# A 90-degree rotation on one core: in twelve macro tiles, two neighbouring outputs are stored by one 4 MB transfer

## The chip, the core and the metric

The kernel runs on one core of a Trainium2 chip. The metric is the time of one launch in microseconds (us); lower is better. A core has five engines with instruction streams of their own: TensorE (PE in the profile; its weight loads are PEld), VectorE (DVE), ScalarE (ACT), GpSimd (POOL) and SyncE (SP). Transfers between DRAM and the on-chip memory SBUF are carried by 16 DMA engines, whichever engine issued them. An engine that issues a transfer goes on; the transfer adds 16 to a semaphore when all of it has landed.

## The reference

```python
def setup_inputs():
    return {"x": np.random.randn(8192, 8192).astype(np.float32), "k": 1}

def reference(x, k):
    return np.rot90(x, k)
```

With k = 1 this is a transpose with the order of the rows reversed: out[i, j] = x[j, 8191 - i]. Nothing is calculated; 268 MB are read and 268 MB written.

## The kernel before

The input is cut into 16 macro tiles of 1024 rows by 4096 columns. Macro tile kk is read by eight loads (T = 8), one for each group of 128 rows: 128 partitions with 16 KB each, 2 MB in all. It leaves as eight outputs (J = 8, numbered j), each of 512 columns of the input, that is 512 rows of the result by 1024 columns: 128 partitions with 4 rows of 4 KB each, 2 MB again. Load number m is row group m % 8 of macro tile m // 8, output n is number n % 8 of macro tile n // 8; there are 128 of each. In the last macro tile alone an output covers 4 row groups and 1024 columns, and is written in rows of 2 KB.

Every step has an engine of its own.

- SyncE issues the loads. The first five go to the five buffers of 16 KB per partition; later, two of them (LAND = 2) receive loads and three (OUTS = 3) hold outputs. Load m waits until VectorE has emptied the buffer that it goes to.
- VectorE (line 209) waits for the load to land (line 203) and copies the tile, with the columns of each block reversed, into a ring of 63 slots of 2 KB per partition. The ring holds one macro tile less one slot, so a tile can be copied only after the outputs of the macro tile before have freed its slots: load m needs output m - 8 to be transposed (`s_half`), and for its last block the beginning of output m - 7 (`s_first`).
- TensorE (line 241) transposes 128 by 128 blocks from the ring into PSUM. The PSUM tensors `ps0` and `ps1` hold one half of an output each; a half is used again once ScalarE has copied it (`s_ev`). The first output of each macro tile, j = 0, needs all eight loads; its transposes are ordered by row group, so that it follows the loads as they land.
- ScalarE (line 272) copies the two halves of an output into its output buffer, having waited, before the first half, until the last store from that buffer has landed (line 268). It then issues the store itself (line 277).

The output buffers are used in turn, in ascending order: `LAND + (n + 1) % OUTS`. The last eight outputs go to all five buffers, as no loads are left by then.

`whole_reads` goes over the finished program: where a store's read of a partition is one contiguous stretch, it writes the access pattern as one run. So a store reads 16 KB runs and writes 4 KB rows.

Of the kernel before, what the change touches and what calls it, by code (L numbers as in the profile page):

```python
# [6 lines left out]
P = 128  # L7
# [3 lines left out]
T = R // P  # L11
W = 4096
G = 4
J = W // (G * P)
# [3 lines left out]
CH = G * P  # L18
F = G * R
# [4 lines left out]
H = 2  # L24
LAND = 2
OUTS = 3

LINE = 1024
HEAD = 224
# [20 lines left out]
def slot(kk, t, j):  # L50

    at = t * J + j if kk % 2 == 0 else J + t + j * T
    return (at + kk // 2 * (J + 1)) % SLOTS


def kernel(tc: tile.TileContext, x: bass.AP, k: bass.AP, out: bass.AP):
    nc = tc.nc
# [4 lines left out]
    dt = x.dtype  # L62
    macros = [(r0, c0) for r0 in range(0, N, R) for c0 in range(0, M, W)]
    KK = len(macros)
    n_out = KK * J
# [18 lines left out]
    with tc.tile_critical():  # L84
        head = nc.alloc_sbuf_tensor("head", [P, HEAD], dt)
        ident, scratch = head[:, :P], head[:, P : P + 1]
        bufs = [nc.alloc_sbuf_tensor(f"buf{i}", [P, F], dt) for i in range(LAND + OUTS)]
        ring = nc.alloc_sbuf_tensor("ring", [P, SLOTS * CH], dt)
        for b in bufs:
            assert nc.lookup_mloc(b).addr % LINE == 0  # L90
        ps = [
            nc.alloc_psum_tensor(f"ps{h}", [P, F // H], mybir.dt.float32)
            for h in range(H)
# [2 lines left out]
        s_id = nc.alloc_semaphore("s_id")  # L96
        s_land = [nc.alloc_semaphore(f"s_land{i}") for i in range(LAND + OUTS)]
        s_store = [nc.alloc_semaphore(f"s_store{i}") for i in range(LAND + OUTS)]
        s_rev = nc.alloc_semaphore("s_rev")
# [4 lines left out]
        def load_buf(m):  # L104
            if m < T:
                return m % (LAND + OUTS)
            return LAND + 2 if m == T else (m - T - 1) % LAND

        def out_buf(n):
            e = n - (n_out - J)  # L110
            if e < 0:
                return LAND + (n + 1) % OUTS
            ends = [load_buf(n_load - 2)]
            ends += [LAND + (n_out - J + i + 1) % OUTS for i in range(OUTS)]
            ends += [load_buf(n_load - 1)]
            return ends[e % len(ends)]

# [24 lines left out]
        def runs(kk, t, lo, hi):  # L142

            at = [slot(kk, t, j) for j in range(lo, hi)]
            i = 0
            while i < len(at):
                n = 1
                step = at[i + 1] - at[i] if i + 1 < len(at) else 1
                if step > 0:
                    while i + n < len(at) and at[i + n] - at[i + n - 1] == step:  # L150
                        n += 1
                else:
                    step = 1
                yield lo + i, n, at[i], step
                i += n

        def load(e, m):
            r0, c0 = macros[m // T]
            b = load_buf(m)
            e.dma_start(  # L160
                out=bufs[b][:], in_=x[r0 + m % T * P : r0 + (m % T + 1) * P, c0 : c0 + W]
            ).then_inc(s_land[b], 16)

        def uses_before(n_or_m, buf):
            return sum(buf(i) == buf(n_or_m) for i in range(n_or_m))
# [4 lines left out]
        with nc.Block() as block:  # L170

            @block.gpsimd
            def _(e):
                e.memset(ident, 0.0).then_inc(s_id, 1)  # L174
                e.wait_ge(s_id, 1)
                e.affine_select(  # L176
                    out=ident,
                    in_=ident,
                    compare_op=mybir.AluOpType.not_equal,
                    fill=1.0,  # L180
                    base=0,
                    pattern=[[-1, P]],
                    channel_multiplier=1,
                ).then_inc(s_id, 1)

            @block.sync
            def _(e):
                for m in range(LAND + OUTS, n_load):
                    last = [i for i in range(m) if load_buf(i) == load_buf(m)]
                    e.wait_ge(s_rev, rev[last[-1], J - 1])  # L190
                    load(e, m)
                for b in range(LAND + OUTS):
                    n = sum(out_buf(i) == b for i in range(n_out))
                    if n:
                        e.wait_ge(s_store[b], 16 * n)

            @block.vector
            def _(e):
                for m in range(n_load):
                    kk, t = divmod(m, T)  # L200
                    b = load_buf(m)
                    a = bufs[b][:].rearrange("p (j c) -> p j c", c=CH)
                    e.wait_ge(s_land[b], 16 * (uses_before(m, load_buf) + 1))
                    for lo, hi, wait in pieces[m]:
                        if wait:
                            e.wait_ge(*wait)
                        for j, n, at, step in runs(kk, t, lo, hi):
                            v = ring[:, at * CH : (at + (n - 1) * step + 1) * CH]
                            i = e.tensor_copy(  # L209
                                out=bass.AP(  # L210
                                    tensor=v.tensor,
                                    offset=v.offset,
                                    ap=[v.ap[0], [step * CH, n], [1, CH]],
                                ),
                                in_=a[:, j : j + n, ::-1],
                            )
                        i.then_inc(s_rev, 1)

            @block.tensor
            def _(e):  # L220
                seen = {}

                def wait(sem, n):
                    if seen.get(sem, 0) < n:
                        seen[sem] = n
                        e.wait_ge(sem, n)

                e.wait_ge(s_id, 2)
                for n, (kk, ts, js) in enumerate(outs):
                    blocks = [(j, g) for j in reversed(js) for g in range(G)]  # L230
                    half = len(blocks) // H
                    rows = len(ts) * P

                    def transpose(t, b):
                        j, g = blocks[b]
                        if n:
                            wait(s_ev, H * (n - 1) + b // half + 1)
                        wait(s_rev, rev[kk * T + t, j])
                        at = slot(kk, t, j) * CH + g * P
                        f = b % half * rows + (t - ts[0]) * P  # L240
                        i = e.transpose(  # L241
                            ps[b // half][:, f : f + P], ring[:, at : at + P], ident
                        )
                        if t == ts[-1] and b % half == half - 1:
                            i.then_inc(s_half, 1)
                        elif t == ts[0] and b == len(blocks) - 1:
                            i.then_inc(s_first, 1)

                    order = [(t, b) for b in range(len(blocks)) for t in ts]
                    if js[0] == 0:  # L250
                        order.sort()
                    for t, b in order:
                        transpose(t, b)

            @block.scalar
            def _(e):
                e.wait_ge(s_id, 2)
                e.copy(scratch, ident[:, :1])  # L258
                for n, (kk, ts, js) in enumerate(outs):
                    r0, c0 = macros[kk]  # L260
                    rows = len(ts) * P
                    b = out_buf(n)
                    for h in range(H):
                        if h == 0:
                            stores = uses_before(n, out_buf)
                            loads = [i for i in range(n_load) if load_buf(i) == b]
                            if stores:
                                e.wait_ge(s_store[b], 16 * stores)
                            elif loads:
                                e.wait_ge(s_rev, rev[loads[-1], J - 1])  # L270
                        e.wait_ge(s_half, H * n + h + 1)  # L271
                        e.copy(  # L272
                            bufs[b][:, h * F // H : (h + 1) * F // H], ps[h][:]
                        ).then_inc(s_ev, 1)
                    top = M - c0 - (js[-1] + 1) * CH
                    e.wait_ge(s_ev, H * (n + 1))
                    e.dma_start(  # L277
                        out=out[
                            top : top + len(js) * CH, r0 + ts[0] * P : r0 + ts[0] * P + rows
                        ].rearrange("(g m) f -> m g f", m=P),  # L280
                        in_=bufs[b][:].rearrange("m (g f) -> m g f", f=rows),
                    ).then_inc(s_store[b], 16)


# [33 lines left out]
```

## Time and profile before

| | |
|---|---|
| time, median of 3 runs | 1265.17 us (1265.15 to 1265.67) |
| the profiled execution's own time | 1265.5 us |
| its span | 1263.6 us |
| busy: PE, PEld, DVE, ACT | 693.0, 647.0, 402.9, 467.0 us |
| moved by DMA | 537.48 MB, mean 425 GB/s over the span |
| a load, from issue to landing | 16.8 us (median) |
| a store, from issue to landing | 25.7 us (median) |
| idle of VectorE, most of it waiting for loads | 812.1 us |
| idle of ScalarE, most of it waiting for stores | 778.2 us |

Times in the profile count from the start of the span. "Idle before" is the time in which an engine had nothing running just ahead of a group of instructions, and the arrow names what ended it. A busy engine is one with an instruction running; for a DMA engine, one with a packet under way. A packet is one read descriptor with the rows that it is written to; here a data packet has 16 KB and a semaphore packet 4 bytes. The queue q1 holds the loads issued by SyncE, q10 the stores issued by ScalarE. The trace lists each packet with its queue, start, duration and size; the prediction calls these packet records.

### The profile page before, as it was taken

The page shows a single profiled execution, that of the slowest core. Times are in us where ns is not written, and L with a number is a line of the kernel's source. Part 1 is how long each engine was busy: PE and PEld are TensorE (multiplying, and loading weights), DVE is VectorE, ACT ScalarE, POOL GpSimd, SP SyncE. Part 2 cuts the span into 40 slices and gives each one's busy share as a digit, 9 for nine tenths or more (in the row PEclk, how much of TensorE's full clock was granted, in tenths as well). Part 3 has the DMA queues.
Part 4 walks back from the last instruction along what each step waited for, and adds up shares of the span by engine and source line. Part 5 has one row for each costly group of instructions (what it writes and reads, how often), then busy time and mean ns, then how long its engine had stood idle before and what let it go on. Part 6 is the DMA issues. An engine that isn't in the chain of part 4 may idle for free.

```text
span 1263.6 us, 9359 instructions
## 1 busy us (share of the span) xinstructions
PE 693.0 (55%) x4096; PEld 647.0 (51%) x4096; DVE 402.9 (32%) x313; ACT 467.0 (37%) x258; POOL 0.7 (0%) x6
## 2 busy tenths in 40 slices
PE   1556554665545655566555555555555555556563
PEld 1445454555545545565554554555445554455563
DVE  3323432234323343322342233422234222442210
ACT  0344333433344333433334333343333433434363
POOL 0000000000000000000000000000000000000000
PEclk9987767677677776767767777777776777767787
DMA  9999999999999999999999999999999999999998
GB/s 398 415 429 429 431 426 429 428 430 429 429 428 429 429 428 429 429 428 429 428 430 428 428 429 429 429 429 428 429 429 429 429 430 427 430 429 429 428 421 338
DMA packets 36904, 537.48 MB, mean 425 GB/s; under 512 B 4096, under 2 KB 4096, under 8 KB 4096
## 3 DMA queue, kind: packets, MB, share of 16 engines
q10 hardware_dynamic: 18432, 268.44, 50.0%
q1 hardware_dynamic: 18432, 268.44, 49.8%
q8 instruction: 32, 0.52, 0.2%
q14 instruction: 8, 0.07, 0.0%
HBM read 268.44 MB, written 268.44 MB: 425 GB/s over the span
## 4 chain that ended last, share of the span: by engine, by line
DMA 80%; issue 7%; ACT 5%; DVE 5%; PE 2%; ACTq 0%; SPq 0%
DMA buf<-in_x_dram 64%; DMA out_dram<-buf 16%; ACT buf L272 5%; DVE ring L209 5%; PE ps L241 2%; ACTq L277 0%; ACTq L271 0%; SPq L313 0%; SPq L84 0%
## 5 line engine op out<-in xcount | busy, mean ns | idle before, releaser
L241 PE MATMUL ps<-head,ring 128*128 128x128 f32 x4096 | 693.0, 346 | 550.7 <-ACT buf L272 472.8
L241 PEld LDWEIGHTS ps<-head,ring 128*128 128x128 f32 x4096 | 647.0, 184 | 596.5 <-ACT buf L272 511.5
L272 ACT COPY buf<-ps 128x2048 f32<-128x2048 f32 x256 | 465.5, 1870 | 778.2 <-DMA out_dram<-buf 594.8
L209 DVE COPY ring<-buf 128x512 f32<-128x512 f32 (+7 forms) x313 | 402.9, 1336 | 812.1 <-DMA buf<-in_x_dram 811.7
L258 ACT ACT_TABLE_LOAD x1 | 1.3, 1283 | 0.9 <-SPq L84 0.9
L176 POOL TENSOR_SCALAR_AFFINE_SELECT head<-head 128x128 f32<-128x128 f32 x1 | 0.3, 293 | 0.2 <-POOL head L174 0.2
L174 POOL MEMSET head<- 128x128 f32 x1 | 0.2, 204 | 0.5 <-SPq L84 0.5
L258 ACT COPY head<-head 128x1 f32<-128x1 f32 x1 | 0.2, 191 | 0.0
L299 POOL MEMSET const-bfloat16-1.0<- 128x1 bf16 x1 | 0.1, 101 | 0.0
L299 POOL MEMSET const-uint8-127<- 128x1 uint8 x1 | 0.1, 101 | 0.0
L299 POOL MEMSET const-float32-0.0<- 128x1 f32 x1 | 0.1, 98 | 0.2 <-issue 0.2
L299 POOL MEMSET const-float32-1.0<- 128x1 f32 x1 | 0.1, 98 | 0.0
## 6 DMA issues: line engine op xcount, KB each, us to landing
buf<-in_x_dram SPq DMA_DIRECT2D x128, 2048.0 KB, 16.8
out_dram<-buf ACTq DMA_DIRECT2D x128, 2048.0 KB, 25.7
```

Of the source, the lines that this page charges most:

```text
L174: e.memset(ident, 0.0).then_inc(s_id, 1)
L176: e.affine_select(out=ident, in_=ident, compare_op=mybir.AluOpType.not_equal, fill=1.0, base=0, pattern=[[-1, P]], channel_multiplier=1,). ...
L209: i = e.tensor_copy(out=bass.AP(tensor=v.tensor, offset=v.offset, ap=[v.ap[0], [step * CH, n], [1, CH]],), in_=a[:, j : j + n, ::-1],)
L241: i = e.transpose(ps[b // half][:, f : f + P], ring[:, at : at + P], ident)
L258: e.copy(scratch, ident[:, :1])
L272: e.copy(bufs[b][:, h * F // H : (h + 1) * F // H], ps[h][:]).then_inc(s_ev, 1)
L299: nc = _bacc.Bacc("TRN2", target_bir_lowering=False, num_devices=1)
```

## The change

In macro tiles 2 to 13, one pair of neighbouring outputs per macro tile (2 and 3, or 3 and 4) is stored by one transfer. After the first output of a pair, ScalarE issues no store and goes on to the second; after the second it issues one store of 4 MB. For this the two outputs have to lie side by side in SBUF with the later one first, since the later output is the upper part of the result. So the five buffers become slices of one tensor `room`, and the output buffers are used in descending order. A pair is possible where output n + 1 is in the buffer just below that of output n. The access pattern of such a store has eight rows of 4 KB per partition on the DRAM side; on the SBUF side `whole_reads` makes it one run of 32 KB. Twelve of the 128 outputs' stores fall away and twelve others have twice the size; 116 stores remain.

A paired store adds 16 to the semaphore of the second output's buffer. The table `stored` says, for each output, which semaphore and count mean that it has landed; the copies that use either buffer again wait for that one. `ends_at` holds the final counts for SyncE's waits at the end. The loads, VectorE's and TensorE's instructions stay as they are, in number and order.

```diff
+FROM = 2
+TO = 14
+PAIRS = (2, 3)
...
-        bufs = [nc.alloc_sbuf_tensor(f"buf{i}", [P, F], dt) for i in range(LAND + OUTS)]
+        room = nc.alloc_sbuf_tensor("room", [P, (LAND + OUTS) * F], dt)
+        bufs = [room[:, i * F : (i + 1) * F] for i in range(LAND + OUTS)]
...
-                return LAND + (n + 1) % OUTS
+                return LAND + (OUTS - 2 - n) % OUTS
             ends = [load_buf(n_load - 2)]
-            ends += [LAND + (n_out - J + i + 1) % OUTS for i in range(OUTS)]
+            ends += [LAND + (OUTS - 2 - n_out + J - i) % OUTS for i in range(OUTS)]
...
+        twice = [
+            n
+            for n in range(J * FROM, J * TO)
+            if n % J in PAIRS and out_buf(n + 1) == out_buf(n) - 1
+        ]
+        twice = [n for n in twice if n - 1 not in twice]
+        stored, ends_at = {}, {i: 0 for i in range(LAND + OUTS)}
+        for n in range(n_out):
+            b = out_buf(n)
+            if n not in twice:
+                ends_at[b] += 16
+                stored[n] = (s_store[b], ends_at[b])
+                if n - 1 in twice:
+                    stored[n - 1] = stored[n]
...
-                            stores = uses_before(n, out_buf)
+                            stores = [i for i in range(n) if out_buf(i) == b]
...
-                                e.wait_ge(s_store[b], 16 * stores)
+                                e.wait_ge(*stored[stores[-1]])
...
+                    if n in twice:
+                        continue
+                    two = n - 1 in twice
                     top = M - c0 - (js[-1] + 1) * CH
+                    tall = (len(js) + two) * CH
                     e.wait_ge(s_ev, H * (n + 1))
                     e.dma_start(
                         out=out[
-                            top : top + len(js) * CH, r0 + ts[0] * P : r0 + ts[0] * P + rows
+                            top : top + tall, r0 + ts[0] * P : r0 + ts[0] * P + rows
                         ].rearrange("(g m) f -> m g f", m=P),
-                        in_=bufs[b][:].rearrange("m (g f) -> m g f", f=rows),
+                        in_=room[:, b * F : (b + 1 + two) * F].rearrange(
+                            "m (g f) -> m g f", f=rows
+                        ),
                     ).then_inc(s_store[b], 16)
```

More of the change, by code (lines that the diff above doesn't have):

```diff
@@ L86 @@
         ident, scratch = head[:, :P], head[:, P : P + 1]
-        bufs = [nc.alloc_sbuf_tensor(f"buf{i}", [P, F], dt) for i in range(LAND + OUTS)]
+        room = nc.alloc_sbuf_tensor("room", [P, (LAND + OUTS) * F], dt)
+        bufs = [room[:, i * F : (i + 1) * F] for i in range(LAND + OUTS)]
         ring = nc.alloc_sbuf_tensor("ring", [P, SLOTS * CH], dt)
-        for b in bufs:
-            assert nc.lookup_mloc(b).addr % LINE == 0
+        assert nc.lookup_mloc(room).addr % LINE == 0
         ps = [
@@ L160, in load @@
             e.dma_start(
-                out=bufs[b][:], in_=x[r0 + m % T * P : r0 + (m % T + 1) * P, c0 : c0 + W]
+                out=bufs[b], in_=x[r0 + m % T * P : r0 + (m % T + 1) * P, c0 : c0 + W]
             ).then_inc(s_land[b], 16)
+        twice = [
[12 more added lines that the diff above has]
+                    stored[n - 1] = stored[n]
         def uses_before(n_or_m, buf):
@@ L191, in _ @@
                     load(e, m)
-                for b in range(LAND + OUTS):
-                    n = sum(out_buf(i) == b for i in range(n_out))
+                for b, n in ends_at.items():
                     if n:
-                        e.wait_ge(s_store[b], 16 * n)
+                        e.wait_ge(s_store[b], n)
             @block.vector
@@ L201, in _ @@
                     b = load_buf(m)
-                    a = bufs[b][:].rearrange("p (j c) -> p j c", c=CH)
+                    a = bufs[b].rearrange("p (j c) -> p j c", c=CH)
                     e.wait_ge(s_land[b], 16 * (uses_before(m, load_buf) + 1))
```

## The prediction

> **What bounds the kernel now.** I read the share of busy time first, then the DMA lines, the waits, a timeline of one macro tile's start, and last the packet records of the trace. No compute engine is over 55% busy. The DMA engines are:
>
> ```profile
> DMA  9999999999999999999999999999999999999998
> GB/s 398 415 429 429 431 426 429 428 430 429 429 428 429 429 428 429 429 428 429 428 430 428 428 429 429 429 429 428 429 429 429 429 430 427 430 429 429 428 421 338
> ...
> q10 hardware_dynamic: 18432, 268.44, 50.0%
> q1 hardware_dynamic: 18432, 268.44, 49.8%
> ```
>
> The 16 DMA engines are busy in every slice at 429 GB/s. q1 carries the loads, q10 the stores. The waits say the same: VectorE waits for loads and ScalarE for stores to free a buffer.
>
> ```profile
> DVE ring L209 <- DMA buf<-in_x_dram: 811.7, 128, 8.4
> ACT buf L272 <- DMA out_dram<-buf: 594.8, 102, 7.1
> ```
>
> So the span is the sum of what each DMA engine works through, and a change counts only if it alters the time per byte or leaves an engine with nothing to do. 18,432 packets per queue are 128 transfers of 128 data records of 16 KB, 8 on each engine, and 16 semaphore records. The packet records give typical durations of 611 ns for a load record, 615 ns for a store record that is written as four 4 KB rows, 626 ns for one of the last macro tile that is written as eight 2 KB rows, and 9 ns for a 4-byte semaphore record. Where both queues have work an engine takes one record from each in turn, whatever its size: even a 9 ns semaphore record uses up its queue's turn. A load and a store record together take 1.22 us, so a 2 MB transfer beside one of the other queue takes 8 x 1.22 = 9.8 us.
>
> **The saving.** The twelve pairs replace 24 stores of 8 records per engine by 12 stores of 8 records of 32 KB. That is 96 records and 12 semaphores fewer on each engine. A record with next to no data costs 9 ns, so the saving is at most 96 x 9 + 12 x 9 ns = 0.97 us. It can be nothing: the number of written rows stays, and the step from 615 to 626 ns shows that rows cost too (11 ns for four). I take 1.0 us. ScalarE's twelve fewer issues (0.55 us each) are off the path, as it idles 778 us.
>
> **What moves: the turns.** If a 32 KB record takes one turn like any other, the stores get two thirds of the engines while a pair is read: 8 turns of 1.23 + 0.61 us = 14.7 us, in which 4 MB of stores but only 2 MB of loads pass. At equal turns that is 19.6 us for the stores, so each pair puts the stores 4.9 us ahead and, against the 9.8 us a load would have needed, the loads 4.9 us behind: 9.8 us apart. Every macro tile has 8 loads and 8 outputs, so this must be given back in each, and it is given back where outputs wait for loads: at the next macro tile's start, whose first output needs the eighth load. Macro tile 5's start now:
>
> ```profile
> 427.42 3.02 DVE L209 COPY ring<-buf 128x512 f32<-128x512 f32 x4 [7.07 <-DMA buf<-in_x_dram]
> 427.90 0.71 PEld L241 LDWEIGHTS ps<-head,ring 128*128 128x128 f32 x4 [3.21 <-DVE ring L209]
> ...
> 428.68 3.63 ACT L272 COPY buf<-ps 128x2048 f32<-128x2048 f32 x2 [8.65 <-PE ps L241]
> ...
> 432.34 0.55 ACTq L277 DMA_DIRECT2D out_dram<-buf  x1
> 435.90 3.63 ACT L272 COPY buf<-ps 128x2048 f32<-128x2048 f32 x2 [3.58 <-DMA out_dram<-buf]
> ...
> 446.02 3.63 ACT L272 COPY buf<-ps 128x2048 f32<-128x2048 f32 x2 [6.49 <-DMA out_dram<-buf]
> ```
>
> Call 427.42 time 0: the macro tile's eighth load is seen. Output 40 goes out at +5.5 (432.34 + 0.55). The last store ahead of it, 39, is seen landed at +18.6 (446.02, which waited for it). To compare these I need two delays, both from the first store of the program, an estimate each: its issue ends at 47.80 and the first load record that it disturbs starts at 49.43, so it reaches the engines after 1.6 us; its own first record starts at 52.41, about three records later, so a record is read some 1.8 us before it is written and, with its 0.6 us and 1.1 us until an engine sees it, 3.5 us before it is seen. The store queue thus needs its next record at 18.6 - 3.5 + 1.2 = +16.3 and has it at 5.5 + 1.6 = +7.1: 9.2 us to spare. The pair of macro tile 2 uses 9.8 of it. From macro tile 4's start on, eleven starts (4 to 14), the store queue must run dry: in balance 4.9 us each, since in that time the loads, alone, gain the 9.8 us back.
>
> **Do the loads fill that gap?** In balance the store queue is dry from +2.2 to +7.1. The ninth load is read from -2.3: 3.7 of its 8 records by +2.2 in turns, the other 4.3 alone at 0.61 us, to +4.8. The tenth is issued after VectorE's 3.02 us and 0.5 us of issue, and the first load of the program took 0.7 us from issue to its first record: +4.2. It is there 0.6 us before it is needed, so nothing stands still; with the whole 9.8 us in one gap (every second start) the ninth would end at +2.6 and 1.6 us would be idle. I take 0 and keep 1.6.
>
> **Other waits.** A pair's two buffers come free together, and the first of the two outputs is stored one output later. Behind ScalarE's wait for the pair stand the copies of the next outputs, and TensorE behind these. The pair is issued 3.63 + 0.56 us after store n-2 is seen and reaches the engines 1.6 us later, at 5.8; the queue needs it at 9.8 - 2.3 = 7.5. After the pair the next store again has 5.8 against 7.5, as output n+2 lies in between, and the one behind it about 11.5 against 17.3 (TensorE's 5.4 us and one more copy). Both at no cost, with 1.7 us of cover; past that the loads would run alone as above. Descending buffers only rename who waits for whom: nothing.
>
> **Price of a restart.** A store queue that ran dry starts up again beside running loads. The trace has that once, at the first store:
>
> ```profile
> 45.00:49.00 4.00, 3.60 (x20) 3.60 (x21) 1.91 (x1) 2.11 (x2) 0.00 (x0) 1.00 1.01 434
> 49.00:53.00 4.00, 2.35 (x22) 2.11 (x21) 0.81 (x2) 2.75 (x2) 0.00 (x0) 1.00 0.97 299
> 53.00:57.00 4.00, 3.42 (x32) 3.13 (x31) 2.62 (x2) 3.32 (x3) 0.00 (x0) 1.00 1.04 446
> ```
>
> The last column is GB/s. From 49 to 57 it averages 372.5 against 431: 8 x 58.5/431 = 1.1 us lost; two or three load records per engine were stretched, to as much as 1.36 us. The other end is nothing: single missed turns of either queue, which occur all through the trace, stretch no record. Between them stands the first load, whose first record took 1.29 us instead of 0.61: 0.7 us. The gaps here are long ones on the store queue, nearest to the first store; but that was also the first of all, so I take 0.9. Eleven starts: 9.9 us. Sum: +9.9 - 1.0 = +8.9 us. The profiled execution, 1265.5 us with a span of 1263.6 (1.9 us lie around it), goes to 1274.4; it stands 0.3 us above the median 1265.17, which goes to **1274.1 us**.
>
> **A rule that says otherwise.** If transfers cost a fixed time of their own, fewer of them would be a gain. Between two transfers of one queue the engines here show a 9 ns semaphore record and go on with the other queue. The most a start costs in these rows is the 0.7 us of the first load, with nothing else running; twelve of them and the 1.0 us would give 1265.2 - 8.4 - 1.0 = 1255.8 us. The Trainium skill (SBUF — State Buffer, section The DMA setup-cost knee) gives each transfer about 2 us that does not grow with its bytes and advises the largest single transfer; by it the change would save about 24 us. The trace disagrees where queues overlap: 0.2% of the engines' time at most is not q1 or q10.
>
> **Rivals.**
> - *Free restart* (0.30): the loads take over without loss; the row for it are the missed turns. 1265.2 - 1.0 = 1264.2 us, no change that can be told.
> - *Not two thirds* (0.06): a 32 KB read is cut into two records, turns stay equal, nothing is saved or moved: 1265.2 us.
> - *Both queues dry* (0.09): the gap falls on VectorE's turnaround and 1.6 us are idle at each of the eleven starts besides: 1274.1 + 17.6 = 1291.7 us. It decides from the point where the gap exceeds about 6 us (its start before +0.9, so that the ninth load ends before +4.2); for it speaks that the loads have only two buffers, against it the 0.6 us to spare.
> - *Fixed cost per transfer* (0.06): 1255.8 us, on the other side; against it stand full DMA slices.
>
> **Numbers.** The forecast has 0.49. A measurement of this kernel can tell about 0.2%, 2.5 us, from no change. Slower by more: forecast and both-dry, 0.58. Within: free restart and not two thirds, 0.36. Faster: 0.06. The range must hold the free restart, so it begins at 1263.8; upward it takes restarts at 1.1 us and half of the idle 1.6 us, 11 x 1.9 - 1.0 = +19.9, and ends at 1285. The forecast's own range is 1268 (restarts at 0.35 us) to 1285.
>
> **What would show it.** Store records of 32 KB, 1,536 of them, between 1.21 and 1.23 us long, with loads at a third of the bytes meanwhile; at macro starts ScalarE no longer waiting for a store at the second output; stretches of 5 us with load records alone and stretched records where stores resume, GB/s there under 429; the twelve pair stores landing about 15 us after they reach the engines. It is wrong if 16 KB records remain, if the slices stay at 429 throughout, or if the load queue is what runs dry.

## The result and the profile after

The changed kernel takes 1274.7 us (median of 6 runs, 1273.75 to 1279.59) against 1265.22 us before; the ratio of the means is 1.0081, 95% interval 1.007 to 1.0092. All ratios below are of means too. The profiled execution took 1275.14 us with a span of 1273.1 us, 9.5 us more span than before. The forecast of 1274.1 us was met, but by a sum whose large terms do not agree with the traces one by one.

The page of the changed kernel, DMA lines:

```profile
DMA  9999999999999999999999999999999999999998
GB/s 397 419 429 431 429 428 429 429 429 429 426 406 429 429 428 429 405 429 430 429 427 396 429 414 428 429 406 428 423 430 429 420 429 430 433 423 400 430 424 371
DMA packets 35176, 537.48 MB, mean 422 GB/s; under 512 B 3904, under 2 KB 3904, under 8 KB 3904
...
q1 hardware_dynamic: 18432, 268.44, 50.3%
q10 hardware_dynamic: 16704, 268.44, 49.6%
```

Every transferred byte is still there, with 1,728 packets fewer on q10 (1,536 data records and 192 semaphore records). The DMA slices still read 9, but single slices fall to as little as 396 GB/s where before all but the first two and the last two held 426 or more. A slice is 31.8 us.

The turns, from the DMA lines of the changed kernel for 230 to 241 us, while the pair of macro tile 2 is read:

```profile
q10 hardware_dynamic: 97, 3.18, 67.7%
q1 hardware_dynamic: 102, 1.52, 32.3%
```

There are about as many store packets as load packets, with twice the share: a 32 KB record takes one turn, as a 16 KB one does. The records of a pair are read within 14.1 to 14.7 us (forecast 14.7).

The start of macro tile 4 in the changed kernel's timeline:

```profile
356.93 2.43 DVE L227 COPY ring<-room 128x512 f32<-128x512 f32 x3 [5.53 <-DMA room<-in_x_dram]
...
358.19 3.63 ACT L290 COPY room<-ps 128x2048 f32<-128x2048 f32 x2 [24.78 <-PE ps L259]
...
361.74 2.35 DVE L227 COPY ring<-room 128x2560 f32<-128x2560 f32 x2 [2.38 <-DMA room<-in_x_dram]
361.85 0.55 ACTq L299 DMA_DIRECT2D out_dram<-room  x1
363.88 3.64 ACT L290 COPY room<-ps 128x2048 f32<-128x2048 f32 x2 [2.05 <-PE ps L259]
364.88 0.43 DVE L227 COPY ring<-room 128x512 f32<-128x512 f32 x1 [0.79 <-PE ps L259]
```

At the start shown in the prediction, that of macro tile 5, ScalarE waited 8.65 us for the first output and then 3.58 us for a store before the second (at macro tile 4's, 8.78 and 3.59 us). Now it waits 24.78 us for the first and for no store at the second: all stores have long landed. The packet records show no store record on most engines from 356.5 to 367.5 us. Over the whole run its waits have moved accordingly:

```profile
DVE ring L227 <- DMA room<-in_x_dram: 817.9, 128, 11.4
...
ACT room L290 <- DMA out_dram<-room: 400.2, 63, 11.3
ACT room L290 <- PE ps L259: 379.2, 69, 41.0
```

ScalarE waits for stores 63 times instead of 102, and VectorE's longest wait for a load has grown from 8.4 to 11.4 us.

Windows of the changed kernel around four macro tile starts, 4, 5, 6 and 7 (the last column is GB/s):

```profile
354.00:368.00 14.00, 8.82 (x56) 8.15 (x57) 5.21 (x6) 7.28 (x4) 0.00 (x0) 0.65 0.98 371
434.00:448.00 14.00, 10.73 (x68) 9.82 (x68) 7.24 (x6) 9.08 (x5) 0.00 (x0) 0.70 1.01 430
512.00:526.00 14.00, 8.53 (x47) 8.13 (x48) 5.22 (x6) 6.42 (x4) 0.00 (x0) 0.56 0.99 373
592.00:606.00 14.00, 10.17 (x58) 9.53 (x59) 6.72 (x6) 7.43 (x5) 0.00 (x0) 0.62 1.01 431
```

All four hold a gap of the store queue. Two cost nothing, two cost 58 GB/s of 430 for 14 us, 1.9 us each. Counting from the packet records, with a gap a stretch of at least 1 us in which at most 6 of the 16 engines have a store record under way, and its price the time by which the load records around it exceed 611 ns, per engine:

| start of macro tile | 3 | 4 | 5 | 6 | 7 | 8 | 9 | 10 | 11 | 12 | 13 | 14 |
|---|---|---|---|---|---|---|---|---|---|---|---|---|
| gap, us | 3.5 | 11.0 | 5.5 | 11.5 | 6.2 | 12.0 | 7.2 | 9.8 | 7.0 | 8.2 | 6.0 | 12.2 |
| price, us | 0.0 | 1.6 | 0.0 | 1.6 | 0.0 | 2.0 | 1.2 | 1.5 | 0.5 | 0.7 | 0.1 | 1.8 |

The prices add up to about 10.9 us before rounding. The gaps are read off in steps of 0.25 us; one more, of 2.75 us at 938 us, does not lie at a macro tile's start and costs nothing.

It matters where in a gap the stretched records start. At the five long gaps (9.8 us and more) 0.3 to 0.7 us per engine starts earlier than 1.5 us after the end of the issue of the store that ends the gap; by the prediction's estimate of 1.6 us this store does not yet reach the engines then. These are places where a load ends while the next has only just been issued: at macro tile 4's start at 359.38 us, 2.45 us after the eighth load was seen. The other 1.2 us starts after that point, up to the store's first records. That is the size, and the distance from the issue, that the program's first store showed (1.1 us). Over all twelve starts about 2.5 us lies ahead of this point and 8.2 us behind it.

The load after that comes late for another reason too. Its buffer is free only when VectorE has copied the last block of the ninth load, and this copy waits for TensorE (the line with 0.79 us, which ends at 365.31 us): the next load is issued at 365.34 us, 3 us after the issue of the store has ended (361.85 + 0.55 us).

Over the whole trace, load records above 680 ns exceed 611 ns by 12.8 us per engine, against 2.2 us in the kernel before: 10.6 us more, which is the 9.5 us of span with the small saving of the large records (0.4 us, below) and 0.7 us unassigned.

### The profile page after: what moved, and what is told of

It reads as the page before. It is cut to its first block, busy times and chain, and to the rows that moved or that the text cites. A ratio compares the mean times of both kernels' runs of the same rounds, so it can differ in the third digit from the quotient of the medians.

```text
span 1273.1 us, 9347 instructions
## 1 busy us (share of the span) xinstructions
PE 655.6 (52%) x4096; PEld 604.6 (47%) x4096; DVE 403.3 (32%) x313; ACT 468.8 (37%) x258; POOL 0.7 (0%) x6
## 3 DMA queue, kind: packets, MB, share of 16 engines
q1 hardware_dynamic: 18432, 268.44, 50.3%
## 4 chain that ended last, share of the span: by engine, by line
DMA 80%; issue 9%; DVE 6%; ACT 3%; PE 1%; ACTq 0%; SPq 0%
DMA room<-in_x_dram 76%; DVE ring L227 6%; DMA out_dram<-room 4%; ACT room L290 3%; PE ps L259 1%; ACTq L299 0%; ACTq L289 0%; SPq L337 0%; SPq L88 0%
## 5 line engine op out<-in xcount | busy, mean ns | idle before, releaser
L259 PE MATMUL ps<-head,ring 128*128 128x128 f32 x4096 | 655.6, 332 | 598.1 <-ACT room L290 371.9
L259 PEld LDWEIGHTS ps<-head,ring 128*128 128x128 f32 x4096 | 604.6, 175 | 649.0 <-ACT room L290 408.6
L290 ACT COPY room<-ps 128x2048 f32<-128x2048 f32 x256 | 467.3, 1870 | 786.3 <-DMA out_dram<-room 400.2
L227 DVE COPY ring<-room 128x512 f32<-128x512 f32 (+7 forms) x313 | 403.3, 1337 | 823.4 <-DMA room<-in_x_dram 817.9
```

The lines of the kernel that those rows point to most:

```text
L227: i = e.tensor_copy(out=bass.AP(tensor=v.tensor, offset=v.offset, ap=[v.ap[0], [step * CH, n], [1, CH]],), in_=a[:, j : j + n, ::-1],)
L259: i = e.transpose(ps[b // half][:, f : f + P], ring[:, at : at + P], ident)
L290: e.copy(bufs[b][:, h * F // H : (h + 1) * F // H], ps[h][:]).then_inc(s_ev, 1)
```

## The experiments

The question after this result was whether the time goes with each restart of the store queue (as forecast), with loads that run dry in long gaps, or with the held output itself. Times are medians; the kernel before took 1265.26 us beside the first four, 1265.35 us beside the others.

**Two stores for each pair.** The first output is still held back; its store is issued with the second's.

```diff
-            if n not in twice:
-                ends_at[b] += 16
-                stored[n] = (s_store[b], ends_at[b])
-                if n - 1 in twice:
-                    stored[n - 1] = stored[n]
+            ends_at[b] += 16
+            stored[n] = (s_store[b], ends_at[b])
...
+                    for o in ([n - 1, n] if n - 1 in twice else [n]):
+                        ob, ojs = out_buf(o), outs[o][2]
...
+                            in_=bufs[ob].rearrange("m (g f) -> m g f", f=rows),
+                        ).then_inc(s_store[ob], 16)
```

> The pair is held as in the changed kernel (no store after its first output), but after the second output both are stored by two transfers of 2 MB with 16 KB records. Theory A (turns: a 32 KB record takes one turn, the stores get ahead, the store queue must run dry at macro starts, and time is lost where the loads run dry too): equal turns, no store gap over 2 us at macro starts, 1265.2 us within 0.5. Rival B (starting a store queue that was idle for long costs about 1 us, whatever the loads do): no gaps, so 1265.2 us as well. Rival C (the held output and the two buffers that come free together cost the time): 1272 to 1276 us.

1265.61 us, ratio 1.0002 (0.9993 to 1.0011). The held output costs nothing that can be told. A miss: three store gaps of 3.5 to 6.0 us did occur, late in the run, and two of them cost 0.3 us each; why they arise was not followed up.

**One transfer of 4 MB, reads of 16 KB.**

```diff
-                    ap = [ap[0], [1, 1], [1, ap[1][1] * ap[2][1]]]
+                    whole = ap[1][1] * ap[2][1]
+                    ap = [ap[0], [F, whole // F], [1, F]]
```

> One transfer of 4 MB per pair as in the changed kernel, but its SBUF reads are kept in two runs of 16 KB per partition. Theory A and rival B: 16,384 store records of 16 KB, equal turns, 1265.0 to 1265.7 us. Rival C, or a cost of the 4 MB transfer as such: 1272 to 1276 us.

1265.88 us, ratio 1.0007 (0.9998 to 1.0017), a little above the range expected. In its page the number of packets tells that only the semaphore records have become fewer (18,432 - 192), and its DMA lines for the same 230 to 241 us as above show shares near one to one:

```profile
q10 hardware_dynamic: 18240, 268.44, 50.1%
q1 hardware_dynamic: 18432, 268.44, 49.8%
```

```profile
q10 hardware_dynamic: 155, 2.54, 54.2%
q1 hardware_dynamic: 155, 2.20, 46.6%
```

So neither the 4 MB transfer nor the two buffers that come free together cost the 9.5 us: it is the size of the record. Seven store gaps of 3.2 to 5.0 us occur here too, and cost less than 0.1 us each.

**No pairs.**

```diff
-PAIRS = (2, 3)
+PAIRS = ()
```

> The changed kernel without any pair: descending buffers and the one tensor for all buffers remain. All theories: 1265.2 us within 0.5. If the buffers' order or place cost anything, it shows here alone.

1265.48 us, ratio 1.0001 (0.9992 to 1.0011): descending buffers and the common tensor cost nothing.

**Pairs with faster VectorE copies.** From macro tile 1 on VectorE copies a quarter of each block, and the rest of the result is left out.

```diff
-                                    ap=[v.ap[0], [step * CH, n], [1, CH]],
+                                    ap=[v.ap[0], [step * CH, n], [1, CH if kk == 0 else P]],
...
-                                in_=a[:, j : j + n, ::-1],
+                                in_=a[:, j : j + n, ::-1] if kk == 0 else a[:, j : j + n, P - 1 :: -1],
```

> The changed kernel, but from macro tile 1 on VectorE copies only 128 of the 512 columns of each block (the rest of the result is not computed), so a load's buffer is free some 2 to 3 us earlier; pairs, records and turns as in the changed kernel. Theory A: the store gaps at macro starts remain (up to 12 us in one, about 5 us on the mean), but the next load is there in time; the sum of stretched load records falls from 10.6 us per engine above that of the kernel before to under 4, and the time to 1265 to 1268.5 us. Rival B: the gaps remain and each long one still costs 1 to 2 us: 1273 to 1276 us. Rival C: 1272 to 1276 us.

1265.67 us, ratio 1.0004 (0.9994 to 1.0013), with the pairs, the 32 KB records and their shares unchanged. Its windows at the starts of macro tiles 4 and 6:

```profile
354.00:368.00 14.00, 8.70 (x57) 8.02 (x58) 1.81 (x6) 7.28 (x4) 0.00 (x0) 0.66 1.01 430
512.00:526.00 14.00, 10.64 (x68) 9.59 (x68) 1.82 (x6) 8.69 (x5) 0.00 (x0) 0.70 1.01 431
```

VectorE's busy time in these windows falls from 5.2 to 1.8 us and the rate stays at 430. The gaps are still there, though most are shorter: 9.8 us at the first, which costs under 0.1 us here and cost 1.5 us at the same length in the changed kernel (macro tile 10); and 7.2 us at the second, at no cost. Stretched load records sum to 2.7 us, against 12.8. So a restart has no fixed price, at least after gaps of up to 9.8 us, and the price hangs on the loads: with shorter copies a buffer comes free earlier (at macro tile 4's start the next load is issued 0.86 us after the eighth was seen, not 2.45), and both parts of the price go. It is not that VectorE's copies slow the transfers: in the changed kernel's window at macro tile 5 VectorE is busy for 7.24 us at 430 GB/s. This run does not tell by which way the 1.2 us behind the store's issue depend on the loads. VectorE's waits for TensorE, the other thing that holds a buffer, did not become shorter (19.8 us in all, against 5.5).

**Its control, the same without pairs** (`PAIRS = ()` besides).

> The control of the run with the shortened VectorE copies: the same without pairs. Theory A: no store gap over 2 us, the same time as that run within 1 us, 1264.5 to 1265.8 us. If shortening the copies gains more than 2 us by itself, the pairs still cost something there and theory A does not hold in full.

1265.11 us, ratio 0.9999 (0.999 to 1.0008). Shorter copies gain nothing by themselves, and with them the pairs cost 0.6 us between medians, no more than the intervals leave open.

**Two pairs, seven macro tiles apart.**

```diff
-            if n % J in PAIRS and out_buf(n + 1) == out_buf(n) - 1
+            if n // J in (2, 9) and n % J in PAIRS and out_buf(n + 1) == out_buf(n) - 1
```

> Only two pairs, in macro tiles 2 and 9. Theory A: each pair moves stores and loads 9.8 us apart and nothing but a gap of the store queue gives it back, so the first uses the 9.2 us of slack (a gap of at most 4 us at macro tile 3's start, none that long from then to macro tile 9), and the second, seven macro tiles later, makes one gap of 6 to 12 us at macro tile 10's start, which costs 0 to 2 us: 1265 to 1267.2 us, all of it in that one place. Rival D (every pair costs about 0.8 us where it stands, a twelfth of the whole): stretched records near both pairs, 1266.5 to 1267 us. Rival E (the slack grows back by itself within some macro tiles): no gap over 4 us at either start.

1267.82 us, ratio 1.0023 (1.0013 to 1.0032). The windows at the starts of macro tiles 3 and 10:

```profile
278.00:288.00 10.00, 9.70 (x62) 9.47 (x63) 4.00 (x2) 6.48 (x5) 0.00 (x0) 0.72 1.01 431
826.00:840.00 14.00, 8.16 (x50) 7.53 (x51) 5.22 (x6) 7.07 (x4) 0.00 (x0) 0.62 0.90 331
```

At macro tile 3's start there is a gap of 3.2 us that costs nothing, then none over 2.0 us until the second pair, and then 14.5 us at once. That one takes (430 - 331) / 430 x 14 = 3.2 us, 1.8 in stretched records and the rest with engines at a standstill (the share is 0.90). Another 0.4 us goes in a gap of 3.5 us right behind the second pair, 0.2 us at 753 to 755 us, and 0.7 us of load records are stretched at 770 to 775 us, where the second pair's first records are read, in store gaps of no more than 1.5 us. Near the first pair none is stretched. So the shift of a pair is kept for seven macro tiles, as forecast, but the rest is a miss: the time (1267.2 us at most), the gap (12 us at most) and its price (2 us at most) were put too low, and not all of it is in that one place. What stretches the records at 770 us is open; a price where a pair stands is not ruled out there.

**An early small store**, added to the kernel before.

```diff
+                e.dma_start(out=out[:P, :P], in_=ident).then_inc(s_try, 16)
+                e.wait_ge(s_try, 16)
                 e.copy(scratch, ident[:, :1])
```

> The kernel before, with one small store (64 KB) issued at the very start while the loads run, and waited for. It asks why the program's first store stretched load records by 1.1 us when later restarts do not. If it is the first use of the store queue (cold): the stretch between 49 and 53 us is gone, 0.5 to 1.1 us faster. If it is that place (a store that sets in as the ninth load ends): the stretch stays, 1265.2 us.

1265.03 us, ratio 0.9999 (0.9991 to 1.0008). Its windows over the first 2 MB store:

```profile
49.00:53.00 4.00, 3.39 (x18) 3.15 (x17) 1.12 (x2) 1.16 (x1) 0.00 (x0) 1.00 1.00 360
53.00:57.00 4.00, 3.23 (x29) 3.19 (x30) 2.51 (x2) 3.33 (x3) 0.00 (x0) 1.00 1.00 426
```

The loss over these 8 us is 38/431 of them, 0.7 us, where it was 1.1. Stretched load records there sum to 0.6 us per engine, in the traces of the other eight kernels to 0.9 to 1.1. Neither answer fits alone: the early store takes away a part, which may be due to first use, and the larger part stays. What causes that is not shown; the next load had been issued long before (at 40.04 us), so it is not a lack of loads.

## Why the prediction was right or wrong

- **The saving** (1.0 us) was too high. Store records of 32 KB have a median of 1,227 ns, against twice 615: 3 ns for each of the 96, 0.3 us, and 0.1 us of semaphores. A record of twice the bytes in twice the rows takes twice the time; hardly any of it belongs to the record as such.
- **Turns, not bytes.** Right: 67.7% to 32.3%, and gone with 16 KB records. The Trainium skill (DMA: Bandwidth & Descriptors, section Queues, rings and completion order) says that an engine drains a packet of some 9 to 17 descriptors of one queue before it switches. In the records here the queues alternate after every single data record (155 to 155 in the run with 16 KB records, 97 to 102 in the changed kernel).
- **The slack of 9.2 us and its first use.** Right: the first pair leads to a gap of 3.5 us (forecast 0.6) that costs nothing, and the run with two pairs shows that the shift stays until a gap gives it back. The two delays behind it, 1.6 and 1.8 us, hold too: where no load record is stretched, the stores resume 3.5 us after the issue (at macro tile 5's start). The text takes 52.41 us for the start of the program's first store record; the very first starts at 51.53 us, the middle ones of the first sixteen at 52.46.
- **The gaps.** Right in place, wrong in size and pattern. The forecast took the balanced case, 4.9 us at each start; measured are 8.4 us on the mean by the count above (which also takes in the skew between engines), and at the first six starts short and long in turn, 3.5, 11.0, 5.5, 11.5, 6.2, 12.0. The text had this case ("every second start") and set it aside.
- **The loads fill the gap.** This is the step that failed. The forecast took 0 and kept 1.6 us of idle time for a long gap. Five gaps of 9.8 us and more cost 1.5 to 2.0 us each, 8.4 us together; three of 7.0 to 8.2 us cost 2.4 us; the four up to 6.2 us cost 0.1. The limit of about 6 us, from VectorE's and SyncE's turnaround, was in the text; that eight of the twelve starts are beyond it was not. Of these prices some 2.5 us lie where the store cannot yet act, so that the loads alone are short. The prediction itself named a load queue that runs dry as a sign that it is wrong. It followed the loads to the tenth only; the one after it, held up by TensorE as well, it left out.
- **The price of a restart** (0.9 us, eleven times) was wrong as a fixed price: it is nothing at the four short gaps and with the faster copies. But the loss that it was read from does come back: at macro tiles 4, 6, 8, 9, 10 and 14 the stretched records behind the store's issue come to 1.1 to 1.2 us, as at the program's first store, and at 11 and 12 to 0.4 and 0.6. When a restart costs this and when nothing is not shown: at the first store a further load had been issued, so dry loads alone are not the condition.
- **The sum.** +9.9 for restarts and 0 for dry loads stood where some 8.2 and 2.5 belong by the places of the stretched records, at eight starts and not at eleven; -1.0 stood for -0.4. Which part of the 8.2 is due to the loads the runs do not tell, and with the faster copies all of it goes. That the total agrees is chance in good part.
- **Other waits at no cost**: right (the run with two stores). **The fixed cost per transfer**: refuted by the run with 4 MB transfers and 16 KB records, twelve transfers fewer at a ratio of 1.0007. The 24 us estimated from the Trainium skill (SBUF — State Buffer, section The DMA setup-cost knee) do not appear where the queues overlap.
- **Both queues dry** was given 0.09 as a surcharge on top of the restarts, at all eleven starts. Its condition is the one that decides: at the eight starts beyond the limit time is lost, and with loads issued earlier none. Its size and its places were wrong, 1.6 us at eleven starts where 0.3 to 0.7 us of load records are stretched ahead of the store at five.

## What to carry to other kernels

Where two DMA queues share busy engines by turns, the size of a record sets the share: larger records on one side take time from the other side, and if both sides must move the same amount, the difference comes back as a gap in the favoured queue. A full DMA line does not mean that there is slack for this; look at what the other queue can supply alone in that gap, that is at how soon its buffers come free. And when a balance gives even gaps, ask whether it settles there or swings.

## What the runs showed of the hardware that was not expected

A store queue that had run dry for up to 9.8 us started again without loss (under 0.1 us) in the kernel with faster copies. In the changed kernel 1.5 to 2.0 us were lost around each gap of 9.8 us and more: three or four load records per engine were stretched, one of them to 2.07 us, while the DMA busy share still showed 0.98 (371 GB/s). Stretched records count as busy, so the rate tells the loss and the share does not. Why 1.2 us of this start only after the store's issue, and why the first store of the program loses 1.1 us, and 0.7 us even after an early small store, with a further load already issued, is open.
